# One encoder trunk on one core: the up projections take both parts of x as one moving operand

## The chip, the cores and the metric

The kernel runs on one core of one Trainium2 chip. A core has engines that run side by side, each with its own in-order queue: PE multiplies matrices, DVE and ACT work elementwise, POOL does small jobs, SP issues most of the DMAs. They wait for one another by semaphores. PE reads its operands from SBUF, the on-chip memory, and writes to PSUM, eight banks of 2048 bytes in each of 128 partitions. DVE and ACT read and write both. The metric is the time of one execution in microseconds (us); less is better.

## The reference

Two layers on x of 256 x 1024 in float32. What the change touches is the gated MLP, the second half of each layer:

```python
h = _rms_norm(x, norm_ffn_pre[i])
a, b = _split(h @ ffn_w_up[i], (D_FF, D_FF))           # 1024 -> 2 x 2816
a = _dwconv3_centred(a, ffn_conv_w[i], ffn_conv_b[i])
y = (jax.nn.gelu(a, approximate=False) * b) @ ffn_w_down[i]
x = x + _rms_norm(y, norm_ffn_post[i])
```

Ahead of it in each layer stands the token mixing: one input projection, three mixers (a long convolution by FFT, gated linear attention, pooling), their merge and an output projection.

## The kernel before

**Numbers in two parts.** PE multiplies in float32r, which keeps the upper bits of a float32. To hold the accuracy each operand is split: `split` (line 124) makes an upper part h (a rounded copy, on ACT) and a lower part l = x - h (on DVE). A product is then three matmuls, h h, h l and l h, which `mm3` (line 128) adds up in one PSUM bank. `mm` (line 119, in the profile line 120) issues every matmul.

**Weights** come in chunks of 128 x 2048 float32, 71 to a layer, in the order in which they are used. SP loads them into a ring of three raw tiles, ACT makes the upper part in two halves of 1024 columns and DVE the lower ones (`split_upper`, `split_lower`). They live in slots of 4096 bytes, `big`, which all large tiles share: a chunk takes four, and x, activations, filter tables and gains take others. A split runs ahead of its use as far as slots are free (`filler`, line 246). PE frees a chunk's slots when it has used it.

**x** after a norm is two upper and two lower tiles, `xt`, 128 x 4 x 256 each (`xt_alloc`, line 549): x transposed, 4 of 8 rows of blocks in each, so four slots of `big`. `transposes` (line 369) writes them from PSUM. The up projection uses the second x of a layer, `xt2`.

**The up stage** (loop from line 1180). The MLP has 11 pairs of 256 a-columns and 256 b-columns. The b-columns of the first four pairs are made beforehand, in another form; the 11 a-products and the 7 other b-products of a layer go through `two_ftiles` (line 576). It takes one chunk and one PSUM bank, and issues two units of 24 matmuls (`ftile`, line 570): for each of 8 k-blocks the three matmuls of `mm3`, with 128 weight columns stationary and 256 columns of x moving. When both halves are through, post-processing reads the bank. For a: `conv3` (line 586) on each half, that is one ACT pass and two shifted DVE multiply-adds, then a GELU on ACT. For b: a multiplication on DVE and a split into `ys_h` and `ys_l`, which the down projection reads.

**What sets the order.** The code is written in one sequence; `unit` (line 320) issues the matmuls of one piece of work, then the post-processing of the piece before, then steps the side work (`tick`) and splits weights (`filler`) by a counter of cost. A scheduler then lays each engine's queue out from this sequence, dependencies and estimated times, so pieces may stand interleaved. During the up stage of the first layer the side work is the filter of the second layer (`filt`, line 467): an MLP and a transform on PE, with much DVE work between. Slots and banks are given out first in, first out, so a bank comes round after the seven others.

Of the kernel before, what the change touches and what calls it, by code (L numbers as in the profile page):

```python
# [83 lines left out]
@with_exitstack  # L84
def trunk(ctx: ExitStack, tc: tile.TileContext, a: dict, out: bass.AP):
    nc = tc.nc
    cpool = ctx.enter_context(tc.tile_pool(name="cst", bufs=1))
    wpool = ctx.enter_context(tc.tile_pool(name="wts", bufs=3))
    spool = ctx.enter_context(tc.tile_pool(name="slt", bufs=1))
    ppool = ctx.enter_context(tc.tile_pool(name="psm", bufs=1, space=bass.MemoryType.PSUM))  # L90
    big = Slots(spool, "b", 37, 4096)
    sml = Slots(spool, "s", 9, 2048)
    psm = Slots(ppool, "p", 8, 2048)

# [10 lines left out]
    def act(o, i, func=AF.Copy, **kw):  # L105
        ins = nc.scalar.activation(o, i, func, **kw)  # L106
        if func in TABLED:
            tc.stamp_issue_order_token(ins.ins, TOKEN)

    def tt(o, x, y, op):  # L110
        nc.vector.tensor_tensor(out=o, in0=x, in1=y, op=op)  # L111
# [7 lines left out]
    def mm(o, w, x, start, stop):  # L119
        ins = nc.tensor.matmul(o, w, x, start=start, stop=stop).ins  # L120
        if not isinstance(ins, tuple):
            newest["pe"] = ins
# [127 lines left out]
    def weights(n, at, width):  # L250

        half, at = divmod(at, 1024)
        return wh[n][half][:, at:at + width], wl[n][half][:, at:at + width]
# [39 lines left out]
    def start(gen, lift=0):  # L293
        s = Side(gen, lift)
        sides.append(s)
        return s

    def tick():
        for s in list(sides):
            s.step()  # L300
            if s.done:
                sides.remove(s)
# [244 lines left out]
    handles = {}  # L547

    def xt_alloc():
        return ([big.get([P, 4, L], F32R) for _ in range(2)], [big.get([P, 4, L], F32R) for _ in range(2)])  # L550

    def chunk_x_stationary(n, xt, t, o, half, first=None, lows_late=False):

# [14 lines left out]
            mm(o, x[:, k, s], l if m == 1 else h, half == 0 and (k, m) == todo[0], half == 1 and (k, m) == todo[-1])  # L568

    def ftile(n, xt, f, o, width=256, kn=8):  # L570
        xth, xtl = xt
        for k in range(kn):
            h, l = weights(n, k * width + f * P, P)
            mm3(o, h, l, xth[k // 4][:, k % 4, :], xtl[k // 4][:, k % 4, :], k == 0, k == kn - 1)

    def two_ftiles(n, xt, post):
        ps = psm.get([P, 2, L])
        unit([n], lambda: ftile(n, xt, 0, ps[:, 0, :]))

        def fin():  # L580
            post(ps)
            psm.put(ps)

        unit([n], lambda: ftile(n, xt, 1, ps[:, 1, :]), fin, free=n)
# [6 lines left out]
    def layer(i, xt, chains):  # L591
# [4 lines left out]
        def take():  # L596
            n = nxt()
            cur["c"] += 1
            return n
# [466 lines left out]
        def branch(b, ready):  # L1066
            for half in range(2):
                gate = room([P, 2, 512])
                if b == 0:
                    merged.append(gate)  # L1070
                n0, n1 = take(), take()
                for t in range(2):
                    ps = psm.get([P, 512])

                    def post(ps=ps, t=t, gate=gate):
                        act(gate[:, t, :], ps[:], AF.Sigmoid)
                        psm.put(ps)
                    for j, nj in enumerate((n0, n1)):
                        unit([nj, n1 if t else n0], lambda: chunk_x_stationary(nj, xt, t, ps[:], j),
                             post if j else None, free=nj if t else None)  # L1080
                ys = ready()
                n = take()
                if b == 2 and half == 1:
                    flush()
                    big.put(*xt[0], *xt[1])
                if b == 2:
                    mhl[half] = big.get([P, 4, L], F32R), big.get([P, 4, L], F32R)
                for t in range(2):
                    ps = psm.get([P, 512])

                    def post(ps=ps, gate=gate, half=half, t=t):
                        g, m = gate[:, t, :], merged[half][:, t, :]
                        tt(g, g, ps[:], ALU.mult)
                        psm.put(ps)
                        if b > 0:
                            tt(m, m, g, ALU.add)
                            if t == 1:
                                big.put(gate)
                        if b == 2:
                            later.append(lambda: merge_up(half, t))  # L1100

                    def pe(ps=ps, t=t):
                        s = slice(t * P, (t + 1) * P)
                        for k in range(4):
                            h, l = weights(n, k * 512, 512)
                            mm(ps[:], ys[0][:, k, s], h, k == 0, False)
                            mm(ps[:], ys[0][:, k, s], l, False, False)
                            mm(ps[:], ys[1][:, k, s], h, False, k == 3)
                    unit([n], pe, post, free=n if t else None)
# [29 lines left out]
        for t in range(2):  # L1139
            banks = [psm.get([P, 512]) for _ in range(2)]  # L1140
            ready = [False, False]
            ch2.append(start(post_norm(t, banks, g_post_t, g_pre2, *xt2, ready), LIFT))
            for c in range(4):
                def fin(ready=ready, c=c):
                    ready[c // 2] = True
                unit(ns[:c + 1] if t == 0 else ns[c:],
                     lambda: chunk_x_stationary(ns[c], mx, t, banks[c // 2][:], c % 2),
                     fin if c % 2 else None, free=ns[c] if t else None)
                if t == 0 and c == 2:
                    open_window()  # L1150
# [29 lines left out]
        for pair in UP_ORDER:  # L1180
            if pair // 2 not in ys_h:
                ys_h[pair // 2] = big.get([P, 4, L], F32R)
                ys_l[pair // 2] = big.get([P, 4, L], F32R)
            ga = sml.get([P, 2, L])

            def a_post(ps, pair=pair, ga=ga):
                for j in range(2):
                    conv3(ga[:, j, :], ps[:, j, :], i, V_FFC + 4 * (pair * 2 + j))
                act(ga[:], ga[:], AF.Gelu)

            def b_post(ps, pair=pair, ga=ga):
                tt(ga[:], ga[:], ps[:], ALU.mult)
                s = slice((pair % 2) * 2, (pair % 2) * 2 + 2)
                split(ys_h[pair // 2][:, s, :], ys_l[pair // 2][:, s, :], ga[:])
                sml.put(ga)
            two_ftiles(take(), xt2, a_post)
            if pair >= NB:
                two_ftiles(take(), xt2, b_post)
            else:
                ps = psm.get([P, 2, L])  # L1200
                for j in range(2):
                    f = (pair * 2 + j) * P
                    for t in range(2):
                        nc.tensor.transpose(ps[:, j, t * P:(t + 1) * P], bt[t][:, f:f + P], ident[:])  # L1204
                flush()

                def fin(ps=ps, b_post=b_post, pair=pair):
                    b_post(ps)
                    psm.put(ps)
                    if pair == NB - 1:  # L1210
                        big.put(*bt)
                pending.append(fin)
# [32 lines left out]
        for at, (t, c) in enumerate(seq):  # L1245
            if not done_first and c == 1:
                done_first = True
                flush()
                big.put(*xt2[0], *xt2[1])
                xt3 = xt_alloc() if not last else (None, None)  # L1250

            def fin(t=t):
                ch3.append(start(post_norm(t, banks[t], g_post2, None if last else g_cur["pre"], *xt3), LIFT))
            oldest = min(cc for _, cc in seq[at:])
            if t == 0 and c == 7 and not last:
                open_window()
            unit([ns[c], ns[oldest]], lambda: down(t, c), fin if c == 10 else None, free=ns[c] if t else None)
            if t == 1 and (c % 2 or c == 10):
                big.put(ys_h[c // 2], ys_l[c // 2])
        if last:  # L1260
            ready = [False, False]
            ch3.append(start(post_norm(1, banks[1], g_post2, None, *xt3, ready)))
            tail = [(half, c) for half in range(2) for c in range(11 - LEAD, 11)]
            for half, c in tail:
                def fin(half=half):
                    ready[half] = True
                unit([ns[c]], lambda: down(1, c, (half,)), fin if c == 10 else None, cost=1.3)
# [240 lines left out]
```

## Time and profile before

| | |
|---|---|
| time, three runs | 886.0, 884.92, 884.22 us (median 884.92) |
| the profiled execution, its time | 884.6 us |
| its span, first to last instruction | 882.8 us |
| mean granted clock of PE | 0.996 of full speed |
| up stage of the first layer | about 287 to 391 us |
| up stage of the second layer | about 711 to 816 us |
| moved from memory | 161.54 MB read, 184 GB/s over the span |

The profile names instructions by the line that records them and by tiles without buffer numbers: `p` is a PSUM bank, `b` a large slot, `s` a small one, `raw` a chunk as loaded. Since helpers record nearly everything, most matmuls stand under line 120, ACT work under 106, DVE work under 111, 114 and 117. PE's row is the matmuls, PEld the loads of stationary operands, which overlap them. "Idle before" is the time that an engine stood still ahead of a group, with what ended it.

### The profile page before, as it was taken

How to read it: one execution, taken by the hardware profiler on the slowest of the kernel's cores; microseconds unless marked ns; L12 is line 12 of the kernel's file. 1: busy time of each engine (PE TensorE's matmuls, PEld its weight loads, DVE VectorE, ACT ScalarE, POOL GpSimd, SP SyncE). 2: the span in 40 equal slices, each digit the busy share in tenths (PEclk: the TensorE clock that was granted, in tenths of full speed). 3: DMA queues.
4: the chain of work that ended last, by engine and by line, in shares of the span. 5: the costliest groups of instructions: out<-in, count | busy, mean ns of one | idle time of the engine just before them, and what ended most of it. 6: DMA issues, size and time to landing. Idle time of an engine off the chain costs nothing.

```text
span 882.8 us, 13499 instructions
## 1 busy us (share of the span) xinstructions
PE 872.6 (99%) x5381; PEld 783.1 (89%) x5381; DVE 636.0 (72%) x925; ACT 512.4 (58%) x809; POOL 37.4 (4%) x86
## 2 busy tenths in 40 slices
PE   9999999999999999999999999999999999999997
PEld 7899987888888999998889999888888899999885
DVE  7899988766586798665288989876755967776612
ACT  7779666555365776554268865864543665555501
POOL 3000100000010000000010000000000000000000
PEclk9999999999999999999999999999999999999999
DMA  9854535746546446466349453465752674445501
GB/s 319 336 192 170 168 105 190 241 144 238 191 163 244 143 136 246 149 222 226 120 136 338 175 160 131 153 198 177 279 184 81 236 284 143 166 173 199 204 1 48
DMA packets 48431, 163.46 MB, mean 185 GB/s; under 512 B 3442, under 2 KB 29189, under 8 KB 33520
## 3 DMA queue, kind: packets, MB, share of 16 engines
q1 hardware_dynamic: 44352, 151.69, 49.2%
q0 software_dynamic: 4000, 10.90, 3.9%
q8 instruction: 42, 0.69, 0.3%
q14 instruction: 21, 0.17, 0.1%
q10 hardware_dynamic: 16, 0.00, 0.0%
HBM read 161.54 MB, written 1.05 MB: 184 GB/s over the span
## 4 chain that ended last, share of the span: by engine, by line
PE 96%; DVE 2%; DMA 1%; ACT 0%; issue 0%; SPq 0%; DVEq 0%; POOLq 0%; POOL 0%; ACTq 0%
PE p L120 94%; DVE b L111 1%; DMA raw<-in_wts 1%; PE p L374 1%; PE p L1059 0%; PE p L1204 0%; DMA x<-in_x 0%; ACT b L106 0%; PE p L775 0%; PE p L876 0%; PE p L1021 0%; DVE b L114 0%; DVE b L1281 0%; DVE s L111 0%; PE p L1294 0%
## 5 line engine op out<-in xcount | busy, mean ns | idle before, releaser
L120 PE MATMUL p<-b,b 128*128 128x256 f32 (+2 forms) x5022 | 842.1, 328 | 2.6 <-DVE b L111 1.9
L120 PEld LDWEIGHTS p<-b,b 128*128 128x128 f32 x5022 | 740.9, 190 | 85.6 <-DVE b L111 3.4
L111 DVE TENSOR_TENSOR b<-raw,b 128x1024 fp32r<-128x1024 f32 (+2 forms) x288 | 342.2, 1208 | 112.7 <-ACT b L106 55.2
L106 ACT ACTIVATE b<-raw 128x1024 fp32r<-128x1024 f32 (+2 forms) x290 | 292.0, 1041 | 159.3 <-PE p L120 128.3
L111 DVE TENSOR_TENSOR b<-p,b 128x512 f32<-128x512 f32 (+2 forms) x72 | 45.7, 654 | 66.5 <-ACT s L106 44.6
L106 ACT ACTIVATE b<-p 128x512 f32<-128x512 f32 (+3 forms) x90 | 50.1, 571 | 66.0 <-PE p L120 39.6
L106 ACT ACTIVATE s<-p 128x256 f32<-128x256 f32 (+3 forms) x50 | 20.3, 415 | 69.0 <-PE p L120 68.7
L114 DVE SCALAR_TENSOR_TENSOR s<-p,vec,s 128x255 f32<-128x255 f32 x104 | 49.3, 478 | 6.4 <-ACT s L106 5.5
L106 ACT ACTIVATE s<-p,vec 128x256 f32<-128x256 f32 x52 | 28.8, 558 | 19.0 <-DVE s L114 15.4
L106 ACT ACTIVATE s<-s 128x512 f32<-128x512 f32 (+6 forms) x54 | 29.0, 537 | 11.1 <-DVE s L111 5.6
L111 DVE TENSOR_TENSOR b<-s,b 128x512 fp32r<-128x512 f32 (+1 forms) x42 | 28.5, 685 | 6.0 <-ACT b L106 6.0
L106 ACT ACTIVATE b<-s 128x512 fp32r<-128x512 f32 x38 | 23.5, 625 | 9.6 <-DVE s L111 9.5
L111 DVE TENSOR_TENSOR b<-b,b 128x512 f32<-128x512 f32 (+4 forms) x28 | 22.4, 802 | 3.8 <-ACT b L106 3.3
L111 DVE TENSOR_TENSOR b<-b,p 128x512 f32<-128x512 f32 x24 | 16.2, 684 | 8.9 <-PE p L120 8.5
L111 DVE TENSOR_TENSOR s<-s,p 128x512 f32<-128x512 f32 x22 | 15.0, 683 | 8.1 <-ACT s L106 7.7
L106 ACT ACTIVATE b<-b,s 128x128 f32<-128x128 f32 x64 | 20.5, 395 | 0.0
L114 DVE SCALAR_TENSOR_TENSOR b<-p,vec,b 128x255 f32<-128x255 f32 (+1 forms) x40 | 19.1, 477 | 0.4 <-ACT b L106 0.3
L387 POOL TENSOR_TENSOR rstd<-mse,mhalf 128x1 f32<-128x1 f32 x16 | 8.9, 557 | 208.0 <-DVE mse L117 208.0
L106 ACT ACTIVATE b<-p,vec 128x256 f32<-128x256 f32 (+1 forms) x24 | 12.7, 530 | 8.1 <-PE p L120 5.8
L106 ACT ACTIVATE b<-b 1x512 f32<-1x512 f32 (+3 forms) x16 | 12.4, 780 | 4.1 <-DVE b L111 4.1
L106 ACT ACTIVATE s<-x 128x512 f32<-128x512 f32 x12 | 7.6, 633 | 11.6 <-DVE x L114 11.4
L164 POOL DMA_DIRECT2D b<-in_gains x7 | 3.9, 553 | 235.0 <-PE p L120 123.2
(108 smaller groups left out, 319.0 us busy)
## 6 DMA issues: line engine op xcount, KB each, us to landing
raw<-in_wts SPq DMA_DIRECT2D x116, 1024.0 KB, 4.9
raw<-in_wts SPq DMA_DIRECT2D x50, 512.0 KB, 4.7
b<-in_gains POOLq DMA_DIRECT2D x7, 512.0 KB, 4.9
b<-in_dft POOLq DMA_DIRECT2D x4, 512.0 KB, 5.4
raw<-in_wts SPq DMA_DIRECT2D x4, 256.0 KB, 5.4
b<-in_gw POOLq DMA_DIRECT2D x2, 512.0 KB, 6.1
b<-in_fw POOLq DMA_DIRECT2D x2, 512.0 KB, 7.3
b<-in_decay POOLq DMA_DIRECT2D x2, 512.0 KB, 7.6
```

The source lines that it names most:

```text
L106: ins = nc.scalar.activation(o, i, func, **kw)
L111: nc.vector.tensor_tensor(out=o, in0=x, in1=y, op=op)
L114: nc.vector.scalar_tensor_tensor(out=o, in0=x, scalar=s, in1=y, op0=op0, op1=op1)
L120: ins = nc.tensor.matmul(o, w, x, start=start, stop=stop).ins
L164: eng.dma_start(g[:], bass.AP(src.tensor, src.offset + (i * 4 + j) * DM, [[0, P], [1, DM]]))
L374: nc.tensor.transpose(ps[k // 4][:, k % 4, :], h[:, k * P:(k + 1) * P], ident[:])
L387: nc.gpsimd.tensor_tensor(out=r[:], in0=e[:], in1=mhalf[:, 0:1], op=ALU.pow)
```

## The change

1. x gets a pool of its own, `xpool`, the first in SBUF. Its two tiles are 128 x 4 x 2 x 256: for each k-block the 256 columns of the upper part are followed by the 256 of the lower part. `big` has 33 slots instead of 37; the bytes are the same. x is no longer returned to `big` between its uses.
2. In the up stage `two_ftiles` takes the new form (`wide=True`). A product holds two banks, one for each half of its columns. In a first unit the upper weights are stationary and 512 columns move, upper and lower x side by side: columns 0 to 255 of the bank receive h h, 256 to 511 receive h l. In a second unit the lower weights meet the upper x, 256 columns, added to the first half of the bank. So 16 matmuls of 512 and 16 of 256 stand where 48 of 256 stood.
3. The two halves of a bank are added afterwards: ACT copies the h l half to SBUF (`tmp`, a small slot), DVE adds the other half from PSUM. Post-processing then reads `tmp`.

The other products of this kind (in the token mixing) keep the old form and read slices of the new tiles.

```diff
+    xpool = ctx.enter_context(tc.tile_pool(name="xts", bufs=1))
...
-    big = Slots(spool, "b", 37, 4096)
+    big = Slots(spool, "b", 33, 4096)
...
     def xt_alloc():
-        return ([big.get([P, 4, L], F32R) for _ in range(2)], [big.get([P, 4, L], F32R) for _ in range(2)])
+        ts = [xpool.tile([P, 4, 2, L], F32R, tag=f"xt{j}", name=f"xt{j}") for j in range(2)]
+        return ([t[:, :, 0, :] for t in ts], [t[:, :, 1, :] for t in ts], ts)
...
+    def ftiles_wide(n, xt, banks, lows):
+        for f, o in enumerate(banks):
+            for k in range(8):
+                h, l = weights(n, k * 256 + f * P, P)
+                x = xt[2][k // 4][:, k % 4]
+                if lows:
+                    mm(o[:, 0, :], l, x[:, 0, :], False, k == 7)
+                else:
+                    mm(o[:], h, x, k == 0, False)
...
-    def two_ftiles(n, xt, post):
+    def two_ftiles(n, xt, post, wide=False):
+        if wide:
...
+            tmp = sml.get([P, 2, L])
+            banks = [psm.get([P, 2, L]) for _ in range(2)]
+            def out():
+                for f, ps in enumerate(banks):
+                    act(tmp[:, f, :], ps[:, 1, :])
+                    tt(tmp[:, f, :], tmp[:, f, :], ps[:, 0, :], ALU.add)
+                psm.put(*banks)
+                post(tmp)
+                sml.put(tmp)
+            unit([n], lambda: ftiles_wide(n, xt, banks, False), cost=3.6)
+            unit([n], lambda: ftiles_wide(n, xt, banks, True), out, cost=1.9, free=n)
+            return
...
-                    big.put(*xt[0], *xt[1])
...
-            two_ftiles(take(), xt2, a_post)
+            two_ftiles(take(), xt2, a_post, True)
...
-                two_ftiles(take(), xt2, b_post)
+                two_ftiles(take(), xt2, b_post, True)
...
-                big.put(*xt2[0], *xt2[1])
```

Three places show how the queues stand. A row is line, operation, output, inputs and shape; for a matmul the first input is the moving one, the second the stationary one.

PE, second layer, middle of the up stage, before: part of one product, where it passes from the first to the second half of its chunk (`b_673` and `b_674` are upper and lower weights of the first half, `b_675` and `b_676` of the second; `b_601` to `b_604` are x):

```order
L120 MATMUL p_256_7862<-b_601_6744,b_673_7708 128x256
L120 MATMUL p_256_7862<-b_603_6746,b_673_7708 128x256
L120 MATMUL p_256_7862<-b_601_6744,b_674_7709 128x256
L120 MATMUL p_256_7862<-b_602_6745,b_675_7714 128x256
L120 MATMUL p_256_7862<-b_604_6747,b_675_7714 128x256
L120 MATMUL p_256_7862<-b_602_6745,b_676_7715 128x256
```

The same place of the change, one whole product (`b_621`, `b_623` upper weights, `b_622`, `b_624` lower; with buffer numbers, so `p0` and `p2` are the banks):

```order
L121 MATMUL p0_269_7158<-xt0_6551,b14_621_6913 128x512 x4
L121 MATMUL p0_269_7158<-xt1_6552,b0_623_6931 128x512 x4
L121 MATMUL p2_270_7159<-xt0_6551,b14_621_6913 128x512 x4
L121 MATMUL p2_270_7159<-xt1_6552,b0_623_6931 128x512 x4
L121 MATMUL p0_269_7158<-xt0_6551,b1_622_6914 128x256 x4
L121 MATMUL p0_269_7158<-xt1_6552,b8_624_6932 128x256 x4
L121 MATMUL p2_270_7159<-xt0_6551,b1_622_6914 128x256 x4
L121 MATMUL p2_270_7159<-xt1_6552,b8_624_6932 128x256 x4
```

The triples are gone: all wide matmuls of both halves come first, the lower weights last, and two banks are held where one was.

PE, first layer, up stage, where the filter's matmuls (`b_251`/`b10_251` and `s_58` stationary after, `b_259` before) stand between. Before, a product in one bank, then a filter step, then the next product:

```order
L120 MATMUL p_123_3170<-b_228_2479,b_276_3072 128x256
L120 MATMUL p_123_3170<-b_226_2477,b_277_3073 128x256
L120 MATMUL p_124_3237<-b_260_2810,b_259_2808 128x512
L120 MATMUL p_124_3237<-b_261_2811,b_259_2808 128x512
L120 MATMUL p_124_3237<-b_260_2810,b_259_2808 128x512
L120 MATMUL p_125_3251<-b_225_2476,b_278_3147 128x256
L120 MATMUL p_125_3251<-b_227_2478,b_278_3147 128x256
```

The change, in the filter's transform. The row ahead of these is one last matmul of 256 into `p5_128`, and the one ahead of that ends the work on `p7_127`; bank 7's next owner, `p7_136`, stands in the last row:

```order
L121 MATMUL p4_132_3203<-xt0_2467,b16_270_3113 128x512 x4
L121 MATMUL p0_129_3166<-b22_252_2809,b10_251_2807 128x512
L121 MATMUL p4_132_3203<-xt1_2468,b28_272_3119 128x512 x4
L121 MATMUL p4_132_3203<-xt0_2467,b29_271_3114 128x256 x4
L121 MATMUL p4_132_3203<-xt1_2468,b6_273_3120 128x256 x2
L121 MATMUL p0_129_3166<-b25_253_2810,b10_251_2807 128x512
L121 MATMUL p0_129_3166<-b22_252_2809,b10_251_2807 128x512
L121 MATMUL p1_133_3235<-b1_254_2811,b10_251_2807 128x512
L121 MATMUL p4_132_3203<-xt1_2468,b6_273_3120 128x256 x2
L121 MATMUL p1_133_3235<-b31_255_2812,b10_251_2807 128x512
L121 MATMUL p1_133_3235<-b1_254_2811,b10_251_2807 128x512
L121 MATMUL p7_136_3275<-xt0_2467,b9_277_3191 128x512 x4
```

The halves of a product are now apart, other work stands between them, and a bank is taken again after about one product's worth of matmuls.

DVE, second layer, up stage, before: four shifted multiply-adds of an a-product from PSUM, a multiplication by b, splits of weights (from `raw`) and of the result:

```order
L114 SCALAR_TENSOR_TENSOR s_125_7316<-p_245_7317,vec,s_125_7316 128x255 x4
L111 TENSOR_TENSOR s_125_7316<-s_125_7316,p_246_7379 128x512
L111 TENSOR_TENSOR b_668_7576<-raw_7448,b_667_7575 128x1024
L111 TENSOR_TENSOR b_644_7127<-s_125_7316,b_643_7126 128x512
L114 SCALAR_TENSOR_TENSOR s_126_7391<-p_247_7392,vec,s_126_7391 128x255 x4
L111 TENSOR_TENSOR b_672_7649<-raw_7448,b_671_7648 128x1024
```

The same place of the change:

```order
L112 TENSOR_TENSOR s_147_7088<-s_147_7088,p_266_7089 128x256
L112 TENSOR_TENSOR b_630_6997<-s_143_6998,b_629_6996 128x512
L112 TENSOR_TENSOR s_147_7088<-s_147_7088,p_267_7090 128x256
L115 SCALAR_TENSOR_TENSOR s_146_7087<-s_147_7088,vec,s_146_7087 128x255 x4
L112 TENSOR_TENSOR b_652_7317<-raw_7209,b_651_7316 128x1024
L112 TENSOR_TENSOR s_146_7087<-s_146_7087,p_268_7140 128x512
L112 TENSOR_TENSOR s_149_7157<-s_149_7157,p_269_7158 128x256
```

The additions of 128x256 (one for each bank) now stand first, and the shifted multiply-adds read the small tile.

More of the change, by code (lines that the diff above doesn't have):

```diff
@@ L570, in ftile @@
     def ftile(n, xt, f, o, width=256, kn=8):
-        xth, xtl = xt
+        xth, xtl = xt[:2]
         for k in range(kn):
@@ L574, in ftile @@
             mm3(o, h, l, xth[k // 4][:, k % 4, :], xtl[k // 4][:, k % 4, :], k == 0, k == kn - 1)
-    def two_ftiles(n, xt, post):
+    def ftiles_wide(n, xt, banks, lows):
[9 more added lines that the diff above has]
+        if wide:
+            c = 0
+            while not sml.free:
+                tick()
+                c += 1
+                assert c < 500, "no room"
+            tmp = sml.get([P, 2, L])
[10 more added lines that the diff above has]
+            return
         ps = psm.get([P, 2, L])
@@ L1141, in layer @@
             ready = [False, False]
-            ch2.append(start(post_norm(t, banks, g_post_t, g_pre2, *xt2, ready), LIFT))
+            ch2.append(start(post_norm(t, banks, g_post_t, g_pre2, *xt2[:2], ready), LIFT))
             for c in range(4):
@@ L1248, in layer @@
                 flush()
-                big.put(*xt2[0], *xt2[1])
                 xt3 = xt_alloc() if not last else (None, None)
             def fin(t=t):
-                ch3.append(start(post_norm(t, banks[t], g_post2, None if last else g_cur["pre"], *xt3), LIFT))
+                ch3.append(start(post_norm(t, banks[t], g_post2, None if last else g_cur["pre"], *xt3[:2]), LIFT))
             oldest = min(cc for _, cc in seq[at:])
@@ L1261, in layer @@
             ready = [False, False]
-            ch3.append(start(post_norm(1, banks[1], g_post2, None, *xt3, ready)))
+            ch3.append(start(post_norm(1, banks[1], g_post2, None, *xt3[:2], ready)))
             tail = [(half, c) for half in range(2) for c in range(11 - LEAD, 11)]
```

## The prediction

> **What bounds the kernel now.** I read the page first: busy time and the chain that ended last.
>
> ```profile
> span 882.8 us, 13499 instructions
> PE 872.6 (99%) x5381; PEld 783.1 (89%) x5381; DVE 636.0 (72%) x925; ACT 512.4 (58%) x809; POOL 37.4 (4%) x86
> PE 96%; DVE 2%; DMA 1%; ACT 0%; issue 0%; SPq 0%; DVEq 0%; POOLq 0%; POOL 0%; ACTq 0%
> ```
>
> The chain is PE for 96% of the span. A busy PE may hide waits, so next the view of who waits for whom, PE alone. This is all of it:
>
> ```profile
> PE p L120 <- DVE b L111: 1.9, 2, 1.8
> PE p L120 <- DVE rmask L260: 1.2, 1, 1.2
> PE p L120 <- ACT b L106: 0.6, 1, 0.6
> ```
>
> PE waits 3.7 us in all. So the time is the sum of PE's spacings, and a change pays exactly what it takes out of PE's stream, as long as DVE and ACT keep up. The groups of PE, by shape:
>
> ```profile
> L120 PE MATMUL p<-b,b 128*128 128x512 f32 x2040 | 483.3, 393 | 2.6 <-DVE b L111 1.9 <-ACT b L106 0.6
> L120 PE MATMUL p<-b,b 128*128 128x256 f32 x2912 | 359.3, 283 | 0.0
> ```
>
> The means (393 and 283 ns) are from start to end of one matmul, and matmuls overlap. The price is the spacing, which long undisturbed runs in the timeline give (start, length, engine, count; the name is that of the first form in the run):
>
> ```profile
> 776.03 40.60 PE L120 MATMUL p<-b,b 128*128 128x256 f32 x337
> 394.72 51.62 PE L120 MATMUL p<-b,b 128*128 128x512 f32 x227
> 391.06 5.87 PE L120 MATMUL p<-b,b 128*128 128x256 f32 x26
> ```
>
> A run lasts (count - 1) spacings and one full matmul. 256 columns: (40.60 - 0.28)/336 = **120.0 ns**. 512 columns: (51.62 - 0.39)/226 = **226.7 ns**. Twice the columns cost 106.7 ns more, so about 13.3 ns of each matmul do not depend on its width. The third row begins with two of 256 and goes on with 24 of 512 (the up stage ends there): 2 x 0.120 + 23 x 0.2267 + 0.39 = 5.84 us, against 5.87. The switch to the wide form costs some 26 ns.
>
> **The PE term.** A product of one chunk (two_ftiles) is 48 matmuls of 256 columns now: 48 x 0.1200 = 5.760 us. In the new form the upper weights meet both parts of x in one matmul of 512, and the lower weights meet the upper part in one of 256: 16 x 0.2267 + 16 x 0.1200 + one switch of 0.026 = 5.573 us. That is 0.187 us less. Eleven a-products and seven b-products per layer take the new form, 36 in all: **36 x 0.187 = 6.7 us less on PE**. The order shows the same matmuls everywhere else, and 576 fewer in the two up stages; POOL's and SP's rows stand in the same order as before, so no DMA moves past another.
>
> A rule speaks against this term. The Trainium skill, "TensorE: Matmul & The Clock Gate", section "Back-to-back issue gap", gives the warm gap as N/2.4 + 2.5 ns, so its fixed part is 2.5 ns. By that rule 576 pairs made into one save 1.4 us instead of 7.7. The spacings above disagree with it: 120.0 where it gives 109.2, 226.7 where it gives 215.8.
>
> **What is added.** Each product now ends with two copies of a 128x256 half-bank on ACT and two additions on DVE, before its old post-processing. Nearest rows of the page's groups by shape:
>
> ```profile
> L106 ACT ACTIVATE s<-p 128x256 f32<-128x256 f32 x16 | 5.8, 384 | 3.8 <-PE p L120 3.6
> L111 DVE TENSOR_TENSOR b<-p,b 128x256 fp32r<-128x256 f32 x8 | 3.4, 420 | 5.4 <-ACT b L106 5.4
> L114 DVE SCALAR_TENSOR_TENSOR s<-p,vec,s 128x255 f32<-128x255 f32 x104 | 49.3, 478 | 6.4 <-ACT s L106 5.5
> L114 DVE SCALAR_TENSOR_TENSOR s<-s 128x256 f32<-128x256 f32 x6 | 2.5, 419 | 0.1
> ```
>
> ACT: 72 x 0.384 = 27.6 us. DVE: 72 x 0.420 = 30.2 us; and the 88 shifted products of the a-convolutions read SBUF instead of PSUM, 0.059 us less each by the last two rows, 5.2 us back. Neither is on PE's path by itself. Whether it gets there is decided in the up stages, whose windows read (busy us of PE, PEld, DVE, ACT, POOL, then granted clock, DMA share, GB/s):
>
> ```profile
> 287.50:391.30 103.80, 103.80 (x843) 102.00 (x842) 81.22 (x120) 64.91 (x90) 1.57 (x3) 1.00 0.52 180
> 712.00:816.40 104.40, 104.40 (x874) 104.40 (x873) 73.01 (x98) 59.06 (x79) 0.57 (x1) 1.00 0.53 185
> ```
>
> Per layer DVE gains 18 x 0.84 - 44 x 0.059 = 12.5 us, ACT 18 x 0.768 = 13.8 us, and the stage is to shrink by 3.4 us. Second layer: DVE 85.5 of 101 us, ACT 72.9. First layer: DVE 93.7 of 100.4 us, ACT 78.7. In the second layer the cover is real; what DVE and ACT wait for there, from 741 to 816 us:
>
> ```profile
> L111 DVE TENSOR_TENSOR b<-raw,b 128x1024 fp32r<-128x1024 f32 x23 | 28.1, 1225 | 16.0 <-PE p L120 10.0 <-ACT b L106 6.1
> L106 ACT ACTIVATE b<-raw 128x1024 fp32r<-128x1024 f32 x24 | 24.9, 1053 | 22.0 <-PE p L120 22.0
> ```
>
> The splitting of weights waits for PE to free slots, so it is as far ahead as the slots allow. By the code late in the stage 37 slots less 4 of x and 12 of y leave 21, five chunks of four; at 5.76 us each I estimate the splits 20 us or more ahead. Stall there: none. The new order also keeps 11 us or more of PE work between a bank's last product and its next use in the second layer (two products).
>
> **The place that can hurt** is the first half of the first layer's up stage, where the next layer's filter runs on DVE too. Five slices of it:
>
> ```profile
> 287.00:297.00 10.00, 10.00 (x81) 9.54 (x81) 8.44 (x17) 7.32 (x11) 0.00 (x0) 1.00 0.49 165
> 297.00:307.00 10.00, 10.00 (x79) 9.65 (x78) 7.06 (x11) 7.32 (x10) 0.00 (x0) 1.00 0.41 152
> 307.00:317.00 10.00, 10.00 (x82) 9.87 (x82) 10.00 (x17) 6.94 (x13) 0.00 (x0) 1.00 0.31 105
> 317.00:327.00 10.00, 10.00 (x75) 9.15 (x74) 10.00 (x15) 8.64 (x13) 0.52 (x1) 1.00 0.31 107
> 327.00:337.00 10.00, 10.00 (x86) 10.00 (x86) 8.74 (x13) 6.43 (x8) 0.00 (x0) 1.00 0.86 313
> ...
> L114 DVE SCALAR_TENSOR_TENSOR s<-p,vec,s 128x255 f32<-128x255 f32 x22 | 10.0, 476 | 0.4 <-ACT s L106 0.4
> ```
>
> DVE is busy 44.2 of these 50 us, 20 of them without a gap. Its 22 shifted products there (last row, four to a convolution pair) make 5.5 a-products, and the order has two b-products among them: 7.5. They add 7.5 x 0.84 - 22 x 0.059 = 5.0 us, so 49.2 us of DVE work meet 50 - 7.5 x 0.187 = 48.6 us of PE work. If the added work fills all of DVE's 5.8 us of gaps, DVE is 0.6 us late at the end. If it fills none, it is 6.4 us late. And here lateness reaches PE: a product holds two PSUM banks until its additions are through, and the filter takes banks between them. In the new order p7_136 begins 14 matmuls of 512 and 9 of 256 after p7_127, the former owner of its bank, ended: 14 x 0.2267 + 9 x 0.120 = 4.3 us in which copy and addition must have had their turn. PE's queue is strict there: behind the waiting product stand the filter's and all other matmuls. **Ends: 0 to 6.4 us of new waiting; I take 1.0**, near the lower end, since the gaps are spread over the same products that bring the additions.
>
> **Edits that I cost at nothing.** The pool of x takes 4 slots out of 37, and x held 4 all along but for the moments between its release and the next claim; PE waited 1.9 + 0.6 us for b tiles in the whole run, and the order of splits up to the first up stage is unchanged but for one exchange on DVE. If a split were late there, it costs PE that wait alone, at most about one split (1.2 us) per layer. The writes of x are strided wider, same shapes: nothing to a gain or loss I can see in any row. The counter behind ticks runs at 5.5 instead of 5.2 a product: side work comes a little earlier, no engine gains or loses an instruction by it.
>
> **Sum.** The profiled execution took 884.6 us, 1.8 us more than its span. 884.6 - 6.7 + 1.0 = 878.9; the median of the runs lies 0.3 above the profiled one: **879.2 us**.
>
> **Rivals.** (1) DVE's gaps cannot be used: waiting of 3 to 6.4 us in the first layer, 881.2 to 884.6. For it: DVE without a gap from 307 to 327. Against: the second layer would still give its 3.4 us, and additions are short. Chance 0.15, four fifths of it below 883.15. (2) Slower: the DVE queue locks with PE in both layers. An addition stands behind a split that waits for a slot, the slot is freed by a product that waits for a bank, and the bank by the addition. Price: a split waited 10.0/23 = 0.43 us for PE; 36 x 0.43 = 15.5 us, 893.7. It decides the sign from 0.187 us a product on. Against: five chunks ahead and two products between uses of a bank. 0.03. (3) The wide form costs nearly two narrow ones: all 512-column rows have weights as the moving operand, none has x, and at 256 columns the loads of weights are busy without a gap (the second figure of the second layer's window), so most of the 13.3 ns might belong to them and stay. At 240 ns nothing is saved: 884.92 + 0.9 for switches + 1.0 = 886.8. At 237 ns 576 x 0.003 = 1.7 is saved: 885.1. Against it are both spacings, each measured over hundreds of matmuls. 0.02 and 0.03. The rule of the skill's page above would put the time close to the second of these.
>
> **How the numbers follow.** Forecast (no more than 2.8 us of waiting): 877.4 to 881.0, chance 0.77. The range to 882.5 adds a part of rival 1. A measurement of this kernel can tell about 0.2%, 1.8 us, from no change. Faster: 0.77 + 0.12 = 0.89. Same: 0.03 of rival 1 and 0.03 of rival 3. Slower: 0.02 of rival 3 and 0.03 of rival 2.
>
> **What would show it.** In the timeline of the second up stage a product takes 5.57 us, with wide ones 227 ns apart. PE's waits list ACT or DVE by a total of about 1 us more, all between 287 and 340 us. DVE's group of 128x256 additions has 72 members near 0.42 us. I am wrong if PE waits in the second up stage, if the wide spacing is near 240, or if stages without an up product change length.

## The result, and the profile after

| | before | after |
|---|---|---|
| median of four runs each, same chip | 884.86 us | 877.86 us |
| lowest and highest | 884.22, 886.0 | 876.71, 878.84 |
| the profiled execution, its time | 884.6 | 878.84 |
| its span | 882.8 | 876.8 |

The ratio is 0.9924, 95% interval 0.991 to 0.9937: 7.0 us faster by the medians, against 5.7 predicted (884.92 to 879.2), and 877.86 lies inside the range. The profiled execution of after is the slowest of its four; why it shows only 5.8 us is looked into below. One execution of experiment 3 took 3068.74 us and is left out of the numbers given there.

The page of after, span, busy time and chain:

```profile
span 876.8 us, 12489 instructions
PE 865.9 (99%) x4805; PEld 752.7 (86%) x4805; DVE 658.3 (75%) x997; ACT 534.1 (61%) x881; POOL 37.4 (4%) x86
PE 96%; DVE 1%; DMA 1%; ACT 1%; SPq 0%; issue 0%; DVEq 0%; POOLq 0%; ACTq 0%
```

PE still makes 96% of the chain. It has 576 matmuls fewer, and DVE has 22 us more. Does PE now wait for DVE? All of PE's waits in after:

```profile
PE p L121 <- DVE b L112: 1.9, 1, 1.9
PE p L121 <- DVE rmask L261: 1.2, 1, 1.2
PE p L121 <- ACT b L107: 1.1, 1, 1.1
PE p L1328 <- DVE b L1323: 0.3, 1, 0.3
```

None is new in an up stage: the 1.9 us stand at 135 us, where PE waits 1.8 us in the kernel before too (the last section shows the row of after), and the others lie in the first 12 us. To see which stage gave the time, I take marks that both programs have: the eight transposes that write the first and the second half of x, in PE's timeline (start, length, engine, line). Before, then after:

```profile
264.44 1.04 PE L374 MATMUL p<-ident,b 128*128 128x128 f32 x8
448.45 1.03 PE L374 MATMUL p<-ident,b 128*128 128x128 f32 x8
460.22 1.04 PE L374 MATMUL p<-ident,b 128*128 128x128 f32 x8
696.48 1.04 PE L374 MATMUL p<-ident,b 128*128 128x128 f32 x8
```

```profile
265.25 1.04 PE L375 MATMUL p<-ident,b 128*128 128x128 f32 x8
445.87 1.04 PE L375 MATMUL p<-ident,b 128*128 128x128 f32 x8
457.67 1.03 PE L375 MATMUL p<-ident,b 128*128 128x128 f32 x8
693.91 1.04 PE L375 MATMUL p<-ident,b 128*128 128x128 f32 x8
```

The differences of these starts, and of the last one to the span's end, are the lengths of the stages:

| stage | before | after | difference |
|---|---|---|---|
| up to the first layer's `xt2` | 264.44 | 265.25 | +0.81 |
| first MLP (448.45 - 264.44; 445.87 - 265.25) | 184.01 | 180.62 | -3.39 |
| between the two halves of the next x | 11.77 | 11.80 | +0.03 |
| second mixing | 236.26 | 236.24 | -0.02 |
| second MLP, to the end | 186.32 | 182.89 | -3.43 |

The two MLPs give 6.82 us. The first row takes back 0.81 us in this one execution, in a part where the change moves next to nothing. The two MLPs and the second mixing repeat to 0.2 us in those profiles below that leave PE's work in them as it is, unless PE waits there, so they tell more than the total times do. The first part spreads by 2.8 us; "Why the profiled execution shows 5.8 us" comes back to it.

Now the product itself. Before, three products stand between two groups of transposes in the second up stage; the same place follows for after:

```profile
734.89 17.52 PE L120 MATMUL p<-b,b 128*128 128x256 f32 x144
752.25 0.60 PE L1204 MATMUL p<-ident,b 128*128 128x128 f32 x4
```

```profile
731.53 16.95 PE L121 MATMUL p<-xt,b 128*128 128x512 f32 x96
748.31 0.60 PE L1239 MATMUL p<-ident,b 128*128 128x128 f32 x4
```

From start to start 17.36 us became 16.78, so a product lost 0.58 / 3 = 0.193 us, and 36 products 6.96 us. The groups of the added and the altered work, by shape:

```profile
L107 ACT ACTIVATE s<-p 128x256 f32<-128x256 f32 x88 | 32.3, 376 | 25.0 <-PE p L121 24.5
L112 DVE TENSOR_TENSOR s<-s,p 128x256 f32<-128x256 f32 x72 | 28.5, 413 | 3.6 <-ACT s L107 3.4
L115 DVE SCALAR_TENSOR_TENSOR s<-s,vec,s 128x255 f32<-128x255 f32 x88 | 39.9, 478 | 5.2 <-ACT s L107 5.0
```

The copies (72 of the 88) and the additions last as long as was said, 376 and 413 ns. The shifted multiply-adds did not become cheaper: 478 ns from SBUF, 478 from PSUM before.

### The profile page after: what moved, and what is told of

The parts are those of the page before. It is cut to its first block, busy times and chain, and to the rows that moved or that the text cites. A ratio compares the mean times of both kernels' runs of the same rounds, so it can differ in the third digit from the quotient of the medians.

```text
span 876.8 us, 12489 instructions
## 1 busy us (share of the span) xinstructions
PE 865.9 (99%) x4805; PEld 752.7 (86%) x4805; DVE 658.3 (75%) x997; ACT 534.1 (61%) x881; POOL 37.4 (4%) x86
## 4 chain that ended last, share of the span: by engine, by line
PE 96%; DVE 1%; DMA 1%; ACT 1%; SPq 0%; issue 0%; DVEq 0%; POOLq 0%; ACTq 0%
PE p L121 94%; DVE b L112 1%; DMA x<-in_x 1%; DMA raw<-in_wts 1%; PE p L375 1%; PE p L1095 0%; PE p L1239 0%; ACT b L107 0%; PE p L811 0%; PE p L1057 0%; PE p L912 0%; DVE s L112 0%; PE p L1328 0%; SPq L200 0%; SPq L160 0%
## 5 line engine op out<-in xcount | busy, mean ns | idle before, releaser
L121 PE MATMUL p<-xt,b 128*128 128x256 f32 (+1 forms) x2336 | 352.5, 310 | 0.0
L121 PEld LDWEIGHTS p<-xt,b 128*128 128x128 f32 x2336 | 324.2, 191 | 26.3 <-issue 1.0
L121 PE MATMUL p<-b,b 128*128 128x512 f32 (+1 forms) x1150 | 267.9, 385 | 0.0
L121 PEld LDWEIGHTS p<-b,b 128*128 128x128 f32 x1150 | 209.3, 188 | 41.1 <-issue 0.3
L121 PE MATMUL p<-b,xt 128*128 128x512 f32 x960 | 232.2, 395 | 3.0 <-DVE b L112 1.9
L121 PEld LDWEIGHTS p<-b,xt 128*128 128x128 f32 x960 | 179.1, 189 | 42.2 <-DVE b L112 3.5
L107 ACT ACTIVATE s<-p 128x256 f32<-128x256 f32 (+3 forms) x122 | 46.8, 391 | 84.9 <-PE p L121 84.3
L115 DVE SCALAR_TENSOR_TENSOR s<-s,vec,s 128x255 f32<-128x255 f32 x88 | 39.9, 478 | 5.2 <-ACT s L107 5.0
L112 DVE TENSOR_TENSOR s<-s,p 128x256 f32<-128x256 f32 (+1 forms) x80 | 33.7, 440 | 4.7 <-ACT s L107 4.5
L107 ACT ACTIVATE s<-s,vec 128x256 f32<-128x256 f32 x44 | 24.6, 592 | 3.3 <-DVE s L112 3.3
L112 DVE TENSOR_TENSOR b<-b,b 128x512 f32<-128x512 f32 (+4 forms) x28 | 22.3, 801 | 2.7 <-ACT b L107 2.2
```

What stands on the lines that cost most here:

```text
L115: nc.vector.scalar_tensor_tensor(out=o, in0=x, scalar=s, in1=y, op0=op0, op1=op1)
```

## The experiments

Theory A is the prediction's: all of the gain is the width of PE's matmuls, and what was added lies beside PE. In experiments 3 and 5 the letter A stands for one step of it alone, which the expectation names. Each edit is shown against the changed kernel. Lengths of stages are taken from the same marks as above.

**1. The pool alone.** x in its own pool and 33 slots, but products as before.

```diff
-            two_ftiles(take(), xt2, a_post, True)
+            two_ftiles(take(), xt2, a_post)
...
-                two_ftiles(take(), xt2, b_post, True)
+                two_ftiles(take(), xt2, b_post)
```

> The pool of x alone: x in its interleaved tiles, 33 slots, all products in the old form of 48 matmuls of 256 columns. Theory A (the gain is PE's spacing alone, 36 products x 0.19 us): 884.9 us, within 1 us of the kernel before, products of 5.76 us. Rival B (a part of the gain comes from where x lies or from the slots): 883 us or less, and a spacing at 256 columns other than 120 ns.

883.96 us, ratio to before 1.0003 (0.9991 to 1.0014). Its two MLPs take 184.01 and 186.38 us, against 184.01 and 186.32 before. The four slots fewer and the wider strides of x cost nothing that shows.

**2. Everything but the width.** Two banks, the new order, copies and additions, but two matmuls of 256 in place of each of 512.

```diff
-                    mm(o[:], h, x, k == 0, False)
+                    for m in range(2):
+                        mm(o[:, m, :], h, x[:, m, :], k == 0 and m == 0, False)
```

> The change with its order, its two banks, its copies and additions, but each wide matmul issued as two of 256 columns with the same stationary weights. Theory A: 48 x 0.120 = 5.76 us a product again, 884.9 us within 1 us; the added work and the order cost and gain nothing. Rival C (lower weights needed later, or the order, pays): 883 us or less. Rival D (the additions cost something that the shorter PE time hid): 886.5 us or more.

884.93 us, ratio 1.0006 (0.9992 to 1.002). Its two MLPs take 184.17 and 186.39 us against 184.01 and 186.32 before. Three products between the same two groups of transposes:

```profile
734.22 17.52 PE L121 MATMUL p<-xt,b 128*128 128x256 f32 x144
751.58 0.60 PE L1240 MATMUL p<-ident,b 128*128 128x128 f32 x4
```

That is 17.36 us from start to start, as before. With the additions in and the width out, nothing is left of the gain, and nothing is lost: the 7 us come with the width alone. The marks also settle the two-spacings question of the prediction: from this run to the change the two MLPs lose 7.05 us, 12.2 ns for each of the 576 pairs, switches included. By the formula of "TensorE: Matmul & The Clock Gate" of the Trainium skill, "Back-to-back issue gap", they would, as an estimate, have lost 1.4 us. That section calls its formula the gap of an isolated matmul, which these streams are not.

**3. Copies and additions twice.**

```diff
-                    act(tmp[:, f, :], ps[:, 1, :])
-                    tt(tmp[:, f, :], tmp[:, f, :], ps[:, 0, :], ALU.add)
+                    for _ in range(2):
+                        act(tmp[:, f, :], ps[:, 1, :])
+                        tt(tmp[:, f, :], tmp[:, f, :], ps[:, 0, :], ALU.add)
```

> The change with each copy and each addition made twice (same result): 72 more copies and 72 more additions, about 15.8 us more on DVE and 14 on ACT per layer. This tries how far the cover of the predicted wait reaches. Theory A (DVE late means PE late, as the prediction had it): the first up stage has 92.0 + 15.8 = 107.8 us of DVE work for 100.5 us, so PE waits there 7 us or more, and 0 to 3 in the second: 885 to 890 us. Rival E (splits of weights are so far ahead that DVE can be late by their lead without PE noticing): 878 to 882 us.

882.04 us, ratio to before 0.9977 (0.9967 to 0.9988), so 4.2 us above the change by the medians. The marks of the first MLP and two of PE's rows from its up stage:

```profile
265.90 1.04 PE L375 MATMUL p<-ident,b 128*128 128x128 f32 x8
...
310.38 5.14 PE L121 MATMUL p<-xt,b 128*128 128x512 f32 x26 [0.40 <-DVE s L112]
...
333.43 11.95 PE L121 MATMUL p<-xt,b 128*128 128x512 f32 x64 [1.56 <-DVE s L112]
...
449.62 1.03 PE L375 MATMUL p<-ident,b 128*128 128x128 f32 x8
...
697.67 1.04 PE L375 MATMUL p<-ident,b 128*128 128x128 f32 x8
```

The first MLP grew by 3.10 us, to 183.72; the second (880.6 - 697.67) stayed at 182.93. The span grew by 3.8, the rest of it ahead of the first MLP. PE waits three times in the first up stage, 2.2 us in all, each time for DVE; the longest wait ends with the last of three additions in a row (332.21 to 333.28 us). Theory A had asked for 7 us or more, and the time lies at the upper edge of what rival E gave. So the place that the prediction named, 287 to 340 us, is where a lack of cover shows first, but this much added work doesn't reach it, and twice as much does.

**4. No additions.** ACT copies the first half of a bank, DVE adds nothing, and the result lacks the product of upper weights and lower x.

```diff
-                    act(tmp[:, f, :], ps[:, 1, :])
-                    tt(tmp[:, f, :], tmp[:, f, :], ps[:, 0, :], ALU.add)
+                    act(tmp[:, f, :], ps[:, 0, :])
```

> The change without its additions: ACT copies the first half of each bank, DVE adds nothing, and the product of upper weights with lower x is computed on PE but left out of the result. Everything of PE stays. Theory A (the additions lie wholly beside PE): time of the change, ratio to the kernel before 0.991 to 0.994, 877 to 878.5 us, the same waits of PE. Theory B (the additions cost about the 1.0 us that was predicted, and the gain of the width is larger than 6.7): 1 us less than the change, ratio below 0.9915. DVE's busy time falls by 72 x 0.44 = 32 us to some 626 us either way.

878.23 us, ratio to before 0.9931 (0.9918 to 0.9944), against 0.9924 with the additions. DVE's busy time fell from 658.3 to 635.3 us, by 23.0 and not by the 32 expected: 0.32 us an addition, since the rows of neighbours on DVE overlap (the section on the prediction shows one). The marks:

```profile
263.70 1.04 PE L375 MATMUL p<-ident,b 128*128 128x128 f32 x8
444.28 1.04 PE L375 MATMUL p<-ident,b 128*128 128x128 f32 x8
...
692.46 1.04 PE L375 MATMUL p<-ident,b 128*128 128x128 f32 x8
```

The first MLP takes 180.58 us against 180.62 with the additions, the second 875.3 - 692.46 = 182.84 against 182.89. The additions cost 0.04 and 0.05 us, within the 0.2 us to which the stages repeat.

**5. Each wide matmul as 384 and 128 columns.** This asks what the saved 13.3 ns are: a fixed part of each matmul, or something that depends on how short it is.

```diff
-                    mm(o[:], h, x, k == 0, False)
+                    of, xf = (v.rearrange("p a b -> p (a b)") for v in (o[:], x))
+                    for c in (slice(0, 384), slice(384, 512)):
+                        mm(of[:, c], h, xf[:, c], k == 0 and c.start == 0, False)
```

> Each wide matmul of the change is issued as two with the same stationary weights, of 384 and of 128 columns. The PE work is the same in columns; the number of matmuls is that of the kernel before. From the spacings 120.0 ns (256 columns) and 226.7 ns (512): 106.7 / 256 = 0.417 ns a column and 13.3 ns that do not depend on the width. Theory A, the 13.3 ns belong to each matmul whatever its width: 384 columns 173.3 ns, 128 columns 66.7 ns, together 240.0, as much as two of 256; a product 16 x 0.2400 + 16 x 0.1200 = 5.76 us and some switches, time as with two narrow ones, 884 to 887 us. Theory G, a matmul cannot begin before its stationary operand is loaded, and a load takes about as long as a 128x128 row of the trace of the change is spaced, some 109 ns (four in a run last 0.63 us): a pair costs 173.3 + 109 = 282 ns, 576 x 0.042 = 24 us more, 908 to 912 us.

912.41 us, ratio to before 1.0314 (1.0296 to 1.0332). Three products in the second up stage:

```profile
752.46 19.74 PE L121 MATMUL p<-xt,b 128*128 128x384 f32 x144
772.04 0.60 PE L1241 MATMUL p<-ident,b 128*128 128x128 f32 x4
```

A product takes 19.58 / 3 = 6.53 us. Without the 16 matmuls of 256 (1.92 us) a pair costs 288 ns, where one of 512 costs 226.7 and two of 256 cost 240. A fixed part of each matmul (theory A) would have given 240: it doesn't describe a short one. If 384 columns cost 173.3 ns, those of 128 cost some 115, more than twice what their width gives. That is near the 109 ns of the transposes and what theory G expected. The Trainium skill, "TensorE: Matmul & The Clock Gate", section "LDWEIGHTS (loading the stationary operand)", gives a load of 128 columns as 128 / 1.2 = 107 ns; as an estimate by it, the pair would be 280 ns, and 288 was measured. The loads of stationary operands in the trace (PEld) agree with theory G: in the run of products from 792 to 844 us they start in turn 108.7 and 178.0 ns apart, as they would if a load took 109 ns and could not hide behind the short matmul. Where all matmuls have 256 columns, in the kernel before, loads start 120 ns apart like the matmuls themselves. That the load is the cause was still not isolated: no run made loads shorter.

**6. All products wide.** The mixing's products too, but for two (k).

```diff
-    def two_ftiles(n, xt, post, wide=False):
+    def two_ftiles(n, xt, post, wide=True):
...
-            while not sml.free:
+            while not sml.free or len(psm.free) < 2:
...
-            two_ftiles(take(), xt, qk_post(enb, pair, None))
+            two_ftiles(take(), xt, qk_post(enb, pair, None), False)
```

> The new form in the token mixing too, for all of its products but the two of k (20 more in all). PE's part: 20 x 0.19 = 3.8 us less, 874.1 us, if the added copies and additions are hidden there. DVE is busy 100.6 of 110 us in that stage of the first layer before, and gains about 4 us net per layer for the 10 products with their convolutions; theory A (PE's spacing and nothing else, cover as in the up stage): 873.5 to 875. Rival F (side work of the mixers, which PE drains at its end, gets later by what DVE gains): 876 to 886, with waits of PE near 110 to 135 and 550 to 570 us.

884.32 us, ratio to before 0.9996 (0.9984 to 1.0008): all of the gain is gone. The marks:

```profile
269.02 1.04 PE L375 MATMUL p<-ident,b 128*128 128x128 f32 x8
...
461.44 1.03 PE L375 MATMUL p<-ident,b 128*128 128x128 f32 x8
...
699.95 1.04 PE L375 MATMUL p<-ident,b 128*128 128x128 f32 x8
```

Ten more products of each layer should have given 10 x 0.193 = 1.9 us in each mixing. The first layer's part came out 3.8 us longer instead (269.02 against 265.25), the second mixing 2.3 us (238.51 against 236.24). The MLPs stayed as they were. This is rival F by its time and by one of the two places that it named: PE's new waits are 1.7 us at 557 to 560 us and 5.2 us between 54 and 82 us.

**7. Four more products of each layer wide (x1 and v).** In experiment 6 I read the new waits in the first layer as those of the later products (x0, q), since they stand at 54 us and after.

```diff
-        two_ftiles(take(), xt, hy_post("x1", 0))
-        two_ftiles(take(), xt, hy_post("v", 0))
+        two_ftiles(take(), xt, hy_post("x1", 0), True)
+        two_ftiles(take(), xt, hy_post("v", 0), True)
...
```

> The change, and besides the wide form in four more products of each layer, those ahead of the long convolution (x1 and v), ahead of which the kernel with all products wide showed no new waiting on PE. Theory A (the gain is 0.19 us a product wherever DVE and ACT have room): 8 x 0.19 = 1.5 us less than the change, ratio to the kernel before 0.9907. Theory F (the mixing has no room for two banks a product and 0.84 us more of DVE): the 1.5 us are given back in waits for ACT s or DVE s, ratio 0.992 to 0.995.

886.07 us, ratio to before 1.0014 (1.0005 to 1.0023). Both theories missed: it is 8 us slower than the change by the medians. The profiled execution is the fastest of its eleven and shows 6 of them. PE's timeline and two windows (PE, PEld, DVE, ACT, POOL, granted clock, DMA, GB/s):

```profile
55.03 3.96 PE L121 MATMUL p<-xt,b 128*128 128x256 f32 x21 [1.98 <-DVE s L112]
...
89.20 0.74 PE L811 MATMUL p<-ident,b 128*128 128x128 f32 x4 [3.26 <-DVE b L112]
...
271.47 1.04 PE L375 MATMUL p<-ident,b 128*128 128x128 f32 x8
```

```profile
57.00:61.00 4.00, 4.00 (x18) 3.62 (x17) 3.82 (x9) 1.47 (x3) 0.00 (x0) 0.68 0.00 0
...
92.00:96.00 4.00, 4.00 (x29) 4.00 (x28) 4.00 (x7) 1.39 (x6) 0.00 (x0) 0.78 0.00 0
```

The first layer's part is 6.2 us longer (271.47), and the 0.8 us of four shorter products are lost too. PE waits behind the four wide products, which end at 53 us, and again 36 us later, each time for DVE, which hasn't caught up; and behind both waits the granted clock is low, 0.68 from 57 to 61 us and 0.78 from 92 to 96 us. So my reading of experiment 6 was wrong: the wait that stands at the later products is caused by the earlier ones.

**8. Six more products wide, in the second layer only.**

```diff
-        two_ftiles(take(), xt, hy_post("x1", 0))
+        two_ftiles(take(), xt, hy_post("x1", 0), i == 1)
...
-        two_ftiles(take(), xt, hy_post("x0", 2))
+        two_ftiles(take(), xt, hy_post("x0", 2), i == 1)
```

> The change, and besides the wide form in the six products of the long convolution (x1, v, x0), but in the second layer alone. With x1 and v wide in both layers the first layer lost some 10 us between 44 and 111 us, where DVE of the change is busy 11.5 of 12 us on average; in the second layer, where it is busy 10.0 to 11.3 of 12 us in the same products, PE waited for nothing. Theory A (0.19 us a product wherever DVE has room): 6 x 0.19 = 1.1 us less than the change, no wait of PE in the second layer's mixing, ratio to the kernel before about 0.991. Theory F (the mixing of either layer has no room): PE waits for DVE or ACT between 480 and 575 us, and the 1.1 us are given back or more, ratio 0.992 or above.

875.78 us, ratio to before 0.9915 (0.9896 to 0.9935), the fastest of all. From the times alone it can't be told from the change (0.991 to 0.9937). The marks tell more:

```profile
455.49 1.03 PE L375 MATMUL p<-ident,b 128*128 128x128 f32 x8
...
690.58 1.04 PE L375 MATMUL p<-ident,b 128*128 128x128 f32 x8
```

The second mixing takes 235.09 us against 236.24: 1.15 us less, 6 x 0.192, with no wait of PE in it. Its three windows from 482 to 518 us show that DVE is nearly full all the same:

```profile
482.00:494.00 12.00, 12.00 (x73) 10.71 (x73) 11.70 (x27) 9.54 (x22) 0.57 (x1) 1.00 0.41 136
494.00:506.00 12.00, 12.00 (x73) 10.74 (x72) 11.89 (x27) 12.00 (x32) 0.54 (x1) 1.00 0.62 224
506.00:518.00 12.00, 12.00 (x96) 11.70 (x95) 12.00 (x26) 11.93 (x31) 0.00 (x0) 1.00 0.31 90
```

DVE 11.7 to 12.0 of 12 us, and PE waits for nothing. A full DVE isn't yet a late one.

## Why the prediction was right

**The PE term held.** 0.187 us a product was forecast from two spacings, 0.193 is measured; 6.7 us, against 6.82 in the two MLPs. Experiment 2 shows that this term is the whole gain. In all of the kernels PE's loads of stationary operands (PEld) are as many as its matmuls, 5381 before and 4805 after, so a matmul saved is a load saved too; which of the two carries the 13.3 ns no run tells. To read the 13.3 ns as a part that each matmul has whatever its width describes 256 and 512 columns and fails at 128 (experiment 5).

**The added waiting was mis-sized.** The step "0 to 6.4 us of new waiting; I take 1.0" measured 0: the first MLP gave 3.39 us, as much as the second, and without the additions (experiment 4) it is no shorter. This 1.0 us is most of the 1.3 us by which the change beat the forecast, though four executions that lie 2 us apart can't resolve so little. The reason I gave for a low value, that the gaps lie among the products that bring the additions, was not the one that counted. In slices of the first up stage of after DVE has no gap left for 40 us:

```profile
307.00:317.00 10.00, 10.00 (x59) 8.80 (x58) 10.00 (x19) 6.92 (x13) 0.00 (x0) 1.00 0.39 138
317.00:327.00 10.00, 10.00 (x56) 8.37 (x55) 10.00 (x17) 9.20 (x16) 0.00 (x0) 1.00 0.38 120
327.00:337.00 10.00, 10.00 (x58) 8.74 (x57) 10.00 (x15) 7.00 (x12) 0.52 (x1) 1.00 0.54 198
337.00:347.00 10.00, 10.00 (x64) 9.01 (x64) 9.99 (x19) 8.06 (x13) 0.00 (x0) 1.00 0.87 315
```

So the gaps were filled and PE still did not wait. The mistake was to take DVE's lateness for PE's at once: a full queue holds work that PE needs soon (additions, which free banks) and work that it needs later (splits, which run ahead), and both had room. Additions ended up to 6 us after the last matmul of their bank (331.35 to 337.80 us), and PE still found its banks free. The named place shows how close it came. PE's first matmul on bank 7 again, and the addition that frees that bank by the order of both queues:

```profile
315.01 0.41 DVE L112 TENSOR_TENSOR s<-s,p 128x256 f32<-128x256 f32 x1
```

```profile
316.12 1.07 PE L121 MATMUL p<-xt,b 128*128 128x512 f32 x4
```

The addition ends at 315.42, 0.70 us before PE needs the bank. Twice the copies and additions (experiment 3) cost the stage 3.10 us, and the longest of its waits is for an addition. The splits' lead did not give way: with the splits counted in the order of the chunks and PE's products with them, the lower halves of the first up stage's chunks are made at least 14.6 us before their first use before, 14.9 us in after and 17.1 us in experiment 3. Late in the second layer's stage, for which the prediction estimated 20 us or more, it is 24.9 us before. So what ran out in experiment 3 was the room of the banks, not the lead of the splits.

**The smaller prices.** Copies at 0.384 and additions at 0.420 us were measured at 0.376 and 0.413. But these are lengths of rows, and rows overlap: the addition above starts at 315.01, lasts 0.41, and the next instruction of DVE starts at 315.34. By busy time an addition cost 0.32 us (experiment 4). The 0.059 us less for each shifted product, 5.2 us of DVE, was wrong: I took it from a row of another shape (128x256, one input tile), and the same shape costs 478 ns from either memory. The two errors nearly cancel: DVE's busy time grew by 22.3 us where the prediction's prices make 25.0, and that this is close is luck. It changed nothing, as DVE was not the bound. Pool, slots and order at nothing: right (experiments 1 and 2).

**The rivals.** That DVE's gaps can't be used, and that its queue locks with PE's: PE waits in neither up stage. That 512 columns cost nearly two of 256: 16.78 against 17.36 us for three products, and experiment 2. Of what was to show the forecast right, the shorter product, the 72 additions and the unchanged second mixing came as said, and the part ahead of the first MLP differs by less than its own spread; 1 us more of PE's waits between 287 and 340 us did not.

**Why the profiled execution shows 5.8 us and not 7.0.** It loses 0.8 us ahead of the first MLP, and 0.2 us outside of the span. That part takes 263.07 to 265.90 us in the profiles of before, of the change and of experiments 1 to 5 and 8, in which its products are the same; before happened to be profiled in a middling execution and after in a poor one. Of the 0.8 us, 0.6 arise in the first 12 us, where the second group of eight transposes begins at 11.36 us before and at 11.96 us in after. Much of the spread among the eight profiles is the clock, next, but not this difference: the clock drops at 135 us in both. That the 5.8 us lie beside the forecast's 5.7 is luck.

## What to carry to other kernels

Where PE bounds a kernel and a stationary operand meets two moving ones, laying these side by side saves a price for each matmul saved (here 13.3 of 240 ns), and the price can be read beforehand from the spacings of two widths; at 128 columns it no longer held. What such a form adds on other engines is judged at the place where PE next needs the bank, not by the busy share: DVE without a gap for 40 us cost nothing in the up stage, while four more products in the first mixing made that part 6.2 us longer. To see a gain of one part in a hundred, measure stages between marks that both programs have; here the MLPs and the second mixing repeat to 0.2 us, where whole runs differ by 2.

## What the runs showed of the hardware that I had not expected

**A wait of 1.9 us can cost 3.5.** At about 135 us PE waits 1.75 to 1.92 us for a split in before, in after and in experiments 1 to 5 and 8. Behind it come the same 23 matmuls of 512. In after, the row of the timeline and the window of 134 to 138 us (the clock is the figure ahead of the last two):

```profile
135.10 7.12 PE L121 MATMUL p<-b,xt 128*128 128x512 f32 x23 [1.92 <-DVE b L112]
```

```profile
134.00:138.00 4.00, 2.90 (x7) 2.33 (x8) 4.00 (x7) 1.03 (x2) 0.00 (x0) 0.64 0.44 140
```

The same two in experiment 4:

```profile
135.14 5.53 PE L121 MATMUL p<-b,xt 128*128 128x512 f32 x23 [1.89 <-DVE b L112]
```

```profile
134.00:138.00 4.00, 2.86 (x12) 2.36 (x13) 4.00 (x7) 0.99 (x2) 0.00 (x0) 1.00 0.46 132
```

A wait of 1.92 us was followed by a granted clock of 0.64 and 1.6 us more for the same work; one of 1.89 us by none of this. Of the eight profiles named, the clock drops so in before, in after and in experiment 3, and behind the wait of the other five it doesn't (5.5 us for the 23 matmuls). The Trainium skill, "TensorE: Matmul & The Clock Gate", section "What's actually happening", tells of a window of about 3.4 us that runs freely and of half the clock after an idle one. Free running would explain why the same wait is punished in one execution and not in another; but here a wait of little more than half a window was enough. In experiment 7 the low clock behind its waits adds to the loss. Whole runs differ with the clock too: of the 17 executions of before that were taken beside experiments 4, 5 and 7, the ten with a mean granted clock of 0.996 took 884.61 to 885.8 us, and the seven with 0.998 or 0.999 took 882.94 to 884.34 us.

**A matmul of 128 columns cost about 115 ns** beside one of 384 (experiment 5), if the 384 columns cost what the two spacings give. However the pair divides, cutting one wide matmul at 384 costs 61 ns, and cutting it in the middle 13.
